# An encoder block on one core: the stages of both latents and of latent attention put in an order worked out from a table of lengths, with products of zeros and ScalarE's loads at the start

## The chip, the core and the metric

The kernel runs on one core of one Trainium2 chip. The metric is the device time of one execution in microseconds (us). Five engines work side by side: TensorE (PE: products and transposes; PEld are its weight loads), VectorE (DVE), ScalarE (ACT), GpSimd (POOL) and SyncE (SP), which only issues transfers here. ScalarE and GpSimd issue transfers too. Each engine works through its own list of instructions in order and waits at each one until its inputs are there.

## What is computed

One layer of a residual block over 512 tokens of width 2048, all in F32. The normalised input is projected once; the columns of the projection feed three branches (a gated short convolution, latent attention, attention to 256 memory tokens) and their gates. What the change touches are the two latents and latent attention:

```python
h = rms_norm(x, norm_g[l]);  proj = h @ w_in[l]          # ... c_q (512), c_kv (512), k_rope_raw (64) ...
q  = (rms_norm(c_q, q_norm_g) @ w_uq).reshape(b, s, 16, 128 + 64)
kv = (rms_norm(c_kv, kv_norm_g) @ w_ukv).reshape(b, s, 16, 128 + 128)
# per head: RMS norm of the 128 and of the 64, rotation of the 64, one shared rotated key,
# scores masked by chunks of 64 tokens, softmax, times values
x = x + merged @ w_o[l]
```

## The kernel before

**Products in three parts.** Every F32 operand is split into a rounded part (`hi`) and the rest (`lo`); `mm3` (lines 124 to 129) makes one product out of three: hi by hi, hi by lo, lo by hi. ScalarE writes the rounded part (line 117), VectorE the rest (line 119, or 121 with a gain). So each chunk of weights costs a transfer (SP), one ScalarE and one VectorE instruction (`forms_of`, lines 220 to 232) before TensorE can use it. Weights come through a ring of 10 tiles (tag `w`) and 6 (`wf`). PSUM has eight banks under two tags, `acc` and `aux`, four each.

**The order of the work.** Stages are lists of steps; `run_range` (lines 263 to 273) makes the next step's forms ahead of this step's products. Line 111 takes SP's queue as written. The order on the other engines comes from a scheduler that keeps its own time line when the program is built; it moves instructions freely past each other where no data forbid it.

**The start.** Lines 146 to 155 load the gains and the identity from ScalarE's queue and run one small activation. Then come the key/value latent's two halves (lines 486 to 533: 8 chunks of 288 columns for half 0, then 8 for half 1; half 0 also loads, splits and squares x, `x_chunk` and `x_squares`, lines 466 to 484), the scale of x (`make_scale`, line 537), and the query latent (line 582: 8 chunks of 512 columns, 24 products each). While these run, x is normalised and cut into the blocks of the next stage (`normalize`, `sums_x`, `build`).

**Latent attention.** The memory heads end with lines 1080 to 1085, then the latents are put into blocks. For each of eight groups of two heads, `keys_values` (line 1113) makes keys and values (48 products of 512 columns) and `queries` (line 1135) the queries (48 products of 384 columns), both out of four banks, with sums of squares, inverse roots on GpSimd (line 136) and scaling. `attend` (line 1182) is one head in four parts: transposes of keys and queries with their splits (`feat`, line 1187), scores and softmax (lines 1206 to 1226), transposes of the probabilities with their splits, the product with the values. Parts are interleaved by strings: `p` is a piece of the projection of the next group, `0` and `1` a part of a head, `L` the last part of the group before:

```python
ORDER_FIRST = "ppppp0p0p0p1p1p0p1"
ORDER = "pp0Lppp01pp01pp01p"
ORDER_LAST = "0p0p1pLp0p1p0p1p1"
```

In the last string `p` is half a step of the next stage, the memory branch's output (lines 1326 to 1328); its inputs are reloaded and split by lines 1410 to 1414. The strings set program order only; the scheduler still moves instructions.

**The end.** `out_group` (line 1385) adds the residual; its last block is stored by one transfer of 512 KB (`put`, line 1393).

Of the kernel before, what the change touches and what calls it, by code (L numbers as in the profile page):

```python
# [43 lines left out]

LINE = 512
SMALL_FILL = 56
# [44 lines left out]

def body(ctx, tc, a, out):
    nc = tc.nc
# [55 lines left out]
    nc.scalar.dma_start(ident, a["ident"])  # L149
# [5 lines left out]
    act.activation(one, one, AF.Copy)  # L155
# [306 lines left out]
    open_work(("q", "b1"))  # L462
    xraw, hx = [None] * 8, [None] * KB
    xacc = []

    def x_chunk(c):
        t = xraw[c] = q("xraw")
        hi, lo = (blk("xhi"), blk("xlo")) if c < 4 else (b1("xhi"), b1("xlo"))
        if c == 0:
            for k in range(KC):  # L470
                nc.sync.dma_start(t[:, k], a["xT"][:, k])
        else:
            nc.sync.dma_start(t, a["xT"][:, KC * c:KC * (c + 1)])
        for k in range(KC):
            split(t[:, k], hi[:, k], lo[:, k], g(G_NORM + KC * c + k))
            hx[KC * c + k] = (hi[:, k], lo[:, k])
# [11 lines left out]

    def kv_forms(n, c):
        if n == 0:  # L490
            x_chunk(c)
        raw = w("raw")
        src = a[f"w_ckv{n}"][c]
        for c0 in range(0, 2 * NK, NK if c == 0 else 2 * NK):
            c1 = c0 + (NK if c == 0 else 2 * NK)
            nc.sync.dma_start(flat(raw)[:, c0:c1], src[:, c0:c1])
        r = forms_of(raw, 2 * NK, c == 0)
        w_done()
        return r

    def kv_products(ws, n, c):
        if c == 0:
            banks_kv[n] = [bank("acc" if n else "aux") for _ in range(NTB)]
        hi, lo = (flat(t)[:, :2 * NK].rearrange("p (k n) -> p k n", k=2) for t in ws)
        for i, k in ([(i, k) for k in range(KC) for i in range(NTB)] if c == 0 else
                     [(i, k) for i in range(NTB) for k in range(KC)]):
# [23 lines left out]
    for n in range(2):  # L530
        for c in range(8):
            steps.append(Step(lambda n=n, c=c: kv_forms(n, c), [lambda ws, n=n, c=c: kv_products(ws, n, c)],
                              [lambda n=n: kv_results(n)] if c == 7 else []))
# [42 lines left out]
    for c in range(8):  # L576
        after(c, lambda c=c: x_squares(c))
    after(7, make_scale)
    for c in range(4):
        after(9 + c, lambda c=c: normalize(c))  # L580
    after(13, lambda: sums_x(0))
# [338 lines left out]
    def rotary_tables():  # L920
        pc, pcr = P2["lat"], P2["latrow"]
        tabs = {}
        pos_i = pcr.tile([P, NTB], I32, name="pos_i")
# [130 lines left out]
    run_all(run_range(0, end_m))  # L1054
# [116 lines left out]
    deep[0] = 0  # L1171
    res0 = {}
# [212 lines left out]
    def out_group(grp):  # L1385
        at = block_of(grp)
        xs = {}

        def early(t, n):
            xs[t, n] = q("x")  # L1390
            nc.gpsimd.dma_start(xs[t, n], at(a["x"], t, n))

        def put(t, n, r):
            nc.scalar.dma_start(at(out, t, n), r)

        def direct(x, r):
            for tt in range(2):
                vec.tensor_tensor(out=r[:, tt], in0=x[tt], in1=xs[0, 0][:, tt], op=ALU.add)
            put(0, 0, r)
        return t_results(put, direct, early, lambda t, n: xs[t, n])  # L1400
# [16 lines left out]
    run(*[{"p": late_steps, "L": late, "0": a0, "1": a1}[c] for c in ORDER_LAST])  # L1417
    close_p()
# [101 lines left out]
```

## Time and profile before

| | us |
|---|---|
| median of 3 runs | 2128.02 (2127.25 to 2128.1) |
| the profiled execution | 2125.74 |
| its span, first to last instruction | 2124.0 |
| TensorE busy | 2089.1 (98%) |
| VectorE busy | 1637.6 (77%) |
| ScalarE busy | 1058.5 (50%) |
| GpSimd busy | 146.0 (7%) |

Busy shares are means over stages with different limits, so they are read by stretches. Ends of products are modelled: a product's record can cover a short wait, so a TensorE that counts as busy can still be slower than in a clean stretch. The granted clock of TensorE has two levels, 1.2 and 2.4 GHz; a share of 0.5 of full speed is the lower one.

### The profile page before, as it was taken

Reading aid. Unit: us, or ns where it says so; the run is one execution under the profiler, and the core shown is the slowest. Engines: PE = TensorE matmul, PEld = TensorE weight load, DVE = VectorE, ACT = ScalarE, POOL = GpSimd, SP = SyncE. Lnnn points to the kernel's source line nnn. Section 1 sums busy time; section 2 is a strip of 40 time slices with the busy share of each in tenths; the row PEclk is TensorE's granted clock in tenths of the full one; section 3 lists DMA queues with packets and bytes.
Section 4 is the critical chain, followed back from the end, with each engine's and each line's share of the span. In section 5 each row is a group of like instructions: output and inputs, shape, how many; then the busy total and the mean of one; then the engine's idle time right before and its main releaser. Section 6 shows DMA issues by size and latency. Waiting matters only on the chain.

```text
span 2124.0 us, 28553 instructions
## 1 busy us (share of the span) xinstructions
PE 2089.1 (98%) x10808; PEld 1797.2 (85%) x10808; DVE 1637.6 (77%) x2162; ACT 1058.5 (50%) x1525; POOL 146.0 (7%) x183
## 2 busy tenths in 40 slices
PE   8999999999999999999999999999999999999999
PEld 8888888887899988898888888888888888888887
DVE  6977788788777777777778788768776688867986
ACT  5454354344444444444356576567665344433543
POOL 0000000000000000000000120312211201111000
PEclk9999999999999999999999999999999999999999
DMA  7456445444443446445556654312232667675672
GB/s 250 132 159 200 136 130 156 132 140 143 164 139 121 149 129 197 145 134 160 165 170 199 230 185 141 112 60 87 85 116 86 261 224 207 210 227 179 200 240 76
DMA packets 106442, 338.64 MB, mean 159 GB/s; under 512 B 11072, under 2 KB 11856, under 8 KB 106304
## 3 DMA queue, kind: packets, MB, share of 16 engines
q1 hardware_dynamic: 71792, 252.21, 37.3%
q0 software_dynamic: 13792, 45.57, 7.2%
q10 hardware_dynamic: 20720, 39.04, 4.9%
q8 instruction: 84, 1.38, 0.3%
q14 instruction: 54, 0.44, 0.1%
HBM read 292.61 MB, written 44.17 MB: 159 GB/s over the span
## 4 chain that ended last, share of the span: by engine, by line
PE 93%; DVE 3%; ACT 2%; issue 1%; DMA 1%; SPq 0%; ACTq 0%; DVEq 0%
PE aux L128 15%; PE aux L127 15%; PE aux L129 15%; PE acc L127 14%; PE acc L128 14%; PE acc L129 14%; PE aux L143 1%; DVE wlo L119 1%; ACT whi L117 1%; PE aux L1232 1%; PE aux L1214 0%; PE aux L1212 0%; PE aux L1213 0%; PE aux L1215 0%; PE aux L1216 0%
## 5 line engine op out<-in xcount | busy, mean ns | idle before, releaser
L117 ACT ACTIVATE whi<-raw 128x1024 fp32r<-128x1024 f32 (+2 forms) x614 | 638.2, 1042 | 848.5 <-PE aux L128 366.0
L119 DVE TENSOR_TENSOR wlo<-raw,whi 128x1024 fp32r<-128x1024 f32 (+2 forms) x614 | 733.2, 1200 | 325.3 <-ACT whi L117 320.2
L366 DVE TENSOR_TENSOR raw<-raw 128x1024 f32<-128x1024 f32 x240 | 293.3, 1223 | 11.5 <-DMA raw<-in_w_mla_out 2.8
L128 PE MATMUL aux<-wlo,f 128*128 128x512 f32 x480 | 187.5, 391 | 1.0 <-DVE wlo L119 0.9
L128 PE MATMUL acc<-wlo,b 128*128 128x512 f32 x480 | 187.3, 390 | 0.0
L129 PE MATMUL aux<-whi,f 128*128 128x512 f32 x480 | 186.9, 389 | 0.0
L128 PE MATMUL aux<-wlo,b 128*128 128x512 f32 x480 | 186.8, 389 | 0.0
L129 PE MATMUL acc<-whi,b 128*128 128x512 f32 x480 | 186.8, 389 | 0.0
L129 PE MATMUL aux<-whi,b 128*128 128x512 f32 x480 | 186.8, 389 | 0.0
L127 PE MATMUL aux<-whi,f 128*128 128x512 f32 x480 | 170.2, 390 | 0.0
L127 PE MATMUL acc<-whi,b 128*128 128x512 f32 x480 | 169.0, 390 | 0.8 <-ACT whi L117 0.7
L127 PE MATMUL aux<-whi,b 128*128 128x512 f32 x480 | 168.1, 390 | 1.4 <-ACT whi L117 1.4
L128 PEld LDWEIGHTS aux<-wlo,f 128*128 128x128 f32 x480 | 90.1, 188 | 21.2 <-DVE wlo L119 2.5
L127 PEld LDWEIGHTS aux<-whi,b 128*128 128x128 f32 x480 | 90.0, 188 | 20.8 <-ACT whi L117 2.3
L127 PEld LDWEIGHTS acc<-whi,b 128*128 128x128 f32 x480 | 89.8, 188 | 20.0 <-ACT whi L117 1.6
L128 PEld LDWEIGHTS aux<-wlo,b 128*128 128x128 f32 x480 | 90.1, 188 | 18.8 <-DVE wlo L119 0.2
L129 PEld LDWEIGHTS aux<-whi,b 128*128 128x128 f32 x480 | 90.1, 188 | 18.7
L128 PEld LDWEIGHTS acc<-wlo,b 128*128 128x128 f32 x480 | 90.1, 188 | 18.7 <-DVE wlo L119 0.2
L129 PEld LDWEIGHTS aux<-whi,f 128*128 128x128 f32 x480 | 90.2, 188 | 18.6
L129 PEld LDWEIGHTS acc<-whi,b 128*128 128x128 f32 x480 | 90.1, 188 | 18.5
L127 PEld LDWEIGHTS aux<-whi,f 128*128 128x128 f32 x480 | 89.9, 188 | 18.8 <-ACT E L1373 0.3
L128 PE MATMUL acc<-wlo,f 128*128 128x512 f32 x240 | 93.4, 389 | 0.0
(393 smaller groups left out, 4502.7 us busy)
## 6 DMA issues: line engine op xcount, KB each, us to landing
raw<-in_w_conv SPq DMA_DIRECT2D x80, 512.0 KB, 4.1
raw<-in_w_gmem SPq DMA_DIRECT2D x44, 512.0 KB, 3.8
raw<-in_w_mla_out SPq DMA_DIRECT2D x44, 512.0 KB, 5.1
raw<-in_w_o SPq DMA_DIRECT2D x44, 512.0 KB, 4.4
raw<-in_w_gconv SPq DMA_DIRECT2D x40, 512.0 KB, 4.2
raw<-in_w_gmla SPq DMA_DIRECT2D x40, 512.0 KB, 3.8
raw<-in_w_mlaz SPq DMA_DIRECT2D x32, 512.0 KB, 4.2
raw<-in_w_mem_kv SPq DMA_DIRECT2D x32, 512.0 KB, 4.5
```

The source lines that it names most:

```text
L117: act.activation(hi, src, AF.Copy, scale=1.0 if g is None else g)
L119: vec.tensor_tensor(out=lo, in0=src, in1=r32(hi), op=ALU.subtract)
L127: nc.tensor.matmul(o, lhsT=s[0], rhs=m[0], start=start, stop=False, skip_group_check=shared)
L128: nc.tensor.matmul(o, lhsT=s[0], rhs=m[1], start=False, stop=False, skip_group_check=shared)
L129: nc.tensor.matmul(o, lhsT=s[1], rhs=m[0], start=False, stop=stop, skip_group_check=shared)
L143: nc.tensor.transpose(out=b[:, i * P:(i + 1) * P], in_=s, identity=ident)
L366: vec.tensor_tensor(out=src_, in0=in0, in1=in1, op=op)
L1232: nc.tensor.transpose(out=b[:, i * P:(i + 1) * P], in_=ps[i][:, j * P:(j + 1) * P], identity=ident)
```

## The change

A class `Player` takes the place of the program object. Outside a recording it passes every call on. In a recording (`start` to `play`) each call is kept with a length out of a small table, with what it reads and writes, and with its tiles. `order` then runs through time: of all instructions whose inputs and tiles are there it takes the one that can start first, among equals the one with the lowest priority number (the place in the program of the earliest product that needs it; for those without one, their own place plus `away`). The result is issued in that order on all five engines, under the fixed-order mode that only SP had before. Two stretches are recorded: from the start to the end of the query latent's products (32 further pieces are recorded to know which tiles are still needed, and then issued as before), and from the first queries of latent attention to the end of `ORDER_LAST`.

At the start five products of a cleared F32 tile (256 columns) stand first. ScalarE's queue loads the first weights' halves; the identity and the small activation come after them. Half 0 and half 1 alternate for their first two chunks. Squares of x come two steps later, the scale two steps later, normalising one step later. At the end the last block is stored in two halves as each is ready. `SMALL_FILL` grows by 8 columns and `pos_i` gets a wider tile in another pool.

```diff
+WARM = 5
+START = 32
-SMALL_FILL = 56
+SMALL_FILL = 64
+class Player:
...
+    def order(self, kept, away=0):
+        ops = self.ops
+        for op in reversed(ops):
+            op.prio = min([op.idx + away] + [s.idx if s.eng == "PE" else s.prio for s in op.succs])
+            if op.eng == "PE":
+                op.prio = op.idx
...
+        while len(out) < len(ops):
+            best = None
+            for e, c in ready.items():
+                for op in c:
+                    at = max(clock[e], op.dep)
+                    need = {}
+                    for t in op.gets:
+                        key = self.first[t][1]
+                        n = need.get(key, 0)
+                        if queue[key][n] != t or len(free[key]) <= n:
+                            at = None
+                            break
+                        at = max(at, sorted(free[key])[n])
+                        need[key] = n + 1
+                    if at is None:
+                        continue
+                    rank = (max(at, clock[e] + SLACK), op.prio)
+                    if best is None or rank < best[0]:
+                        best = rank, op, at
...
+        return sorted(out, key=lambda o: o.at)
+    def play(self, tc, kept, rest=0, away=0):
...
+        with tc.manual_schedule(engines={E.PE, E.DVE, E.Activation, E.Pool, E.SP}):
+            for op in out:
+                op.call()
+        for op in later:
+            op.call()
...
+SEM, SLACK, ROOM, LOAD = 0.05, 0.0, 1.18, 0.0016
+def cost(eng, kind, writes, reads):
+    n = max(int(np.prod(a.shape[1:])) for a in (writes[:1] if kind != "tensor_reduce" else reads))
+    if kind == "dma_start":
+        return {"SP": (max(0.45, n * LOAD), 4.5), "ACT": (0.37, 4.5), "POOL": (0.7, 5.0)}[eng]
+    if eng == "PE":
+        occ = 0.109 if kind == "transpose" else max(n, 136) / 2250
+        return occ, occ + 0.25
+    if eng == "ACT":
+        occ = 0.0009 * n + (0.045 if reads[0].space != bass.MemoryType.PSUM else 0.02)
+        occ += 0.09 * (len(reads) > 1) + 0.1 * (len(writes) > 1)
+    elif eng == "DVE":
+        occ = n / 960 + 0.067 + 0.06 * (kind == "scalar_tensor_tensor")
+    else:
+        occ = 0.33 + 0.165 * n
+    return occ * ROOM, occ * ROOM + 0.2
 def body(ctx, tc, a, out):
-    nc = tc.nc
+    nc = Player(tc.nc)
...
-    nc.scalar.dma_start(ident, a["ident"])
-    act.activation(one, one, AF.Copy)
...
     open_work(("q", "b1"))
+    nc.start()
+    warm, wb = q("warm")[:, 0], bank("acc")
+    vec.memset(warm[:, :HS], 0.0)
+    for _ in range(WARM):
+        nc.tensor.matmul(wb[:, :HS], lhsT=warm[:, :P], rhs=warm[:, :HS], start=True, stop=True)
...
+    def first_forms():
+        raw, src = w("raw"), a["w_ckv0"][0]
+        for c0 in (0, NK):
+            nc.scalar.dma_start(flat(raw)[:, c0:c0 + NK], src[:, c0:c0 + NK])
+        nc.scalar.dma_start(ident, a["ident"])
+        act.activation(one, one, AF.Copy)
+        x_load(0)
+        x_split(0, 0)
+        r = forms_of(raw, NK)
+        x_split(0, 1)
+        split(*(flat(t)[:, NK:2 * NK] for t in (raw, *r)))
+        w_done()
+        return r
...
-    for n in range(2):
-        for c in range(8):
+    for n, c in [(n, c) for c in range(2) for n in range(2)] + [(n, c) for n in range(2) for c in range(2, 8)]:
...
-        after(c, lambda c=c: x_squares(c))
-    after(7, make_scale)
+        after(c + 2, lambda c=c: x_squares(c))
+    after(9, make_scale)
...
-        after(9 + c, lambda c=c: normalize(c))
-    after(13, lambda: sums_x(0))
+        after(10 + c, lambda c=c: normalize(c))
+    after(14, lambda: sums_x(0))
...
-    run_all(run_range(0, end_m))
+    early_steps = run_range(0, end_m)
+    for i in range(first + 16 + START):
+        next(early_steps)
+        if i == first + 15:
+            mark = len(nc.ops)
+    nc.play(tc, (), len(nc.ops) - mark, 100)
+    run_all(early_steps)
...
     deep[0] = 0
+    nc.start()
     res0 = {}
     run_all(queries(0, res0))
...
-            put(0, 0, r)
+                nc.scalar.dma_start(at(out, 0, 0)[:, tt], r[:, tt])
...
     run(*[{"p": late_steps, "L": late, "0": a0, "1": a1}[c] for c in ORDER_LAST])
...
+    nc.play(tc, keep)
```

## Rows read from the trace of the kernel before

**Rows 1.** The page: busy time of the engines over the span, and the chain of waits by engine.
```profile
PE 2089.1 (98%) x10808; PEld 1797.2 (85%) x10808; DVE 1637.6 (77%) x2162; ACT 1058.5 (50%) x1525; POOL 146.0 (7%) x183
...
PE 93%; DVE 3%; ACT 2%; issue 1%; DMA 1%; SPq 0%; ACTq 0%; DVEq 0%
```

**Rows 2.** The table by stretches: from and to in us, length, then busy us and number of instructions of PE, PEld, DVE, ACT and POOL, TensorE's granted clock as a share of full speed, the transfer engines' busy share, GB/s.
```profile
5.00:10.00 5.00, 3.10 (x13) 3.10 (x14) 2.85 (x6) 3.45 (x6) 0.00 (x0) 1.00 0.96 340
10.00:15.00 5.00, 4.76 (x31) 4.53 (x31) 4.86 (x7) 5.00 (x9) 0.00 (x0) 1.00 1.03 414
15.00:20.00 5.00, 5.00 (x40) 5.00 (x40) 5.00 (x8) 5.00 (x9) 0.00 (x0) 1.00 1.03 411
...
100.00:200.00 100.00, 100.00 (x443) 82.80 (x442) 77.97 (x70) 48.52 (x51) 0.00 (x0) 1.00 0.55 174
200.00:1000.00 800.00, 796.58 (x4487) 699.46 (x4486) 618.59 (x578) 368.88 (x387) 0.00 (x0) 1.00 0.46 145
```

**Rows 3.** The time line of the first 7 us: start, length, engine (a q marks an engine's issuing of transfers), line, operation, result and sources; in brackets the idle time before it and what ended that.
```profile
0.74 0.42 ACTq L147 DMA_DIRECT2D gains<-in_gains  x1
...
1.19 0.45 ACTq L149 DMA_DIRECT2D ident<-in_ident  x1
...
1.65 0.90 SPq L496 DMA_DIRECT2D raw<-in_w_ckv  x2
1.67 1.28 ACT L155 ACT_TABLE_LOAD   x1 [1.67 <-PEq L1512]
...
4.23 1.33 ACT L117 ACTIVATE xhi<-xraw,gains 128x512 fp32r<-128x512 f32 x2 [1.06 <-DMA gains<-in_gains]
...
5.47 1.04 ACT L480 ACTIVATE sq<-xraw 128x1024 f32<-128x1024 f32 x1
...
6.42 0.43 ACT L117 ACTIVATE whi<-raw 128x288 fp32r<-128x288 f32 x1
...
6.90 1.33 PE L127 MATMUL aux<-whi,xhi 128*128 128x288 f32 x4 [6.90 <-ACT whi L117]
```

**Rows 4.** Transfers: result and source, issuing queue, count, size, us from issue to landing. The first was issued at 1.65 us and the second at 0.74, the third is the last stores (2080 to 2124 us), the fourth a store of half that size at 1397 to 1399 us.
```profile
raw<-in_w_ckv SPq DMA_DIRECT2D x1, 144.0 KB, 3.7
...
gains<-in_gains ACTq DMA_DIRECT2D x1, 35.0 KB, 3.5
...
out<-r ACTq DMA_DIRECT2D x4, 512.0 KB, 2.7
...
adram<-z ACTq DMA_DIRECT2D x1, 256.0 KB, 2.0
```

**Rows 5.** The table by stretches for latent attention as a whole (from the first key/value product to the last product of the last head) and for two clean pieces of it, one of products of 384 columns and one of 256; then a piece of the chain of waits (start, length, engine, tile, line) with 16 transposes.
```profile
1334.28:1657.50 323.22, 304.50 (x1664) 267.43 (x1665) 232.47 (x677) 207.02 (x505) 67.61 (x81) 0.98 0.27 87
1345.28:1351.20 5.92, 5.92 (x35) 5.92 (x34) 4.96 (x16) 2.37 (x8) 2.93 (x4) 1.00 0.71 232
1403.06:1404.26 1.20, 1.20 (x12) 1.15 (x10) 1.17 (x4) 1.16 (x3) 0.00 (x0) 1.00 0.03 10
...
1972.75 1.75 PE aux L143 x16
```

**Rows 6.** The table by stretches from the first heads of latent attention to its last product.
```profile
1360.00:1370.00 10.00, 7.01 (x39) 5.58 (x37) 7.78 (x20) 8.80 (x22) 2.88 (x3) 0.99 0.25 77
1370.00:1380.00 10.00, 9.94 (x43) 8.70 (x44) 9.81 (x36) 4.36 (x13) 4.00 (x4) 0.84 0.18 54
1380.00:1390.00 10.00, 8.13 (x44) 6.40 (x43) 4.86 (x15) 5.86 (x13) 1.41 (x3) 1.00 0.29 93
1390.00:1400.00 10.00, 8.67 (x44) 7.53 (x45) 5.39 (x18) 5.86 (x16) 1.38 (x2) 0.83 0.19 66
1400.00:1540.00 140.00, 135.62 (x783) 120.90 (x782) 109.28 (x329) 96.78 (x240) 32.07 (x38) 1.00 0.25 77
1540.00:1550.00 10.00, 7.62 (x45) 6.37 (x43) 6.01 (x12) 7.05 (x15) 1.52 (x3) 1.00 0.24 87
1550.00:1560.00 10.00, 9.65 (x50) 9.39 (x51) 7.38 (x24) 6.94 (x21) 2.09 (x3) 0.83 0.36 105
1560.00:1640.00 80.00, 77.08 (x429) 67.35 (x427) 57.65 (x158) 49.60 (x114) 13.09 (x15) 1.00 0.32 106
1640.00:1650.00 10.00, 8.71 (x46) 7.74 (x45) 4.77 (x17) 6.57 (x18) 0.55 (x1) 0.83 0.07 27
1650.00:1657.50 7.50, 6.35 (x34) 5.18 (x33) 1.85 (x5) 1.65 (x5) 0.55 (x1) 1.00 0.09 35
```

**Rows 7.** Pieces of the chain of waits in latent attention: start, length, what the chain was in.
```profile
1358.91 2.93 DMA raw<-in_w_uq
...
1466.99 1.07 ACT whi L117
...
1468.09 1.24 DVE wlo L119
...
1469.35 1.23 DVE wlo L119
...
1540.81 3.76 DMA araw<-adram
```

**Rows 8.** The table by stretches for the products of the first queries alone (the tile cqT), the columns as before without GpSimd.
```profile
1308.50:1329.50 21.00, 9.29 (x48) 8.39 (x48) 0.00 (x0) 0.00 (x0) 1.00 0.40 119
```

**Rows 9.** The time line at the end, VectorE: the last addition.
```profile
2119.53 0.69 DVE L1398 TENSOR_TENSOR r<-acc,x 128x512 f32<-128x512 f32 x1 [0.44 <-PE acc L129]
```

More of the change, by code (lines that the diff above doesn't have):

```diff
@@ new lines, with __init__, __getattr__, call @@
+class Queue:
+    def __init__(self, player, real, eng):
+        self.player, self.real, self.eng = player, real, eng
+    def __getattr__(self, kind):
+        f = getattr(self.real, kind)
+        def call(*args, **kw):
+            if self.player.ops is None:
+                return f(*args, **kw)
+            aps = [(k, v) for k, v in list(enumerate(args)) + list(kw.items()) if hasattr(v, "tensor")]
+            writes = [v for k, v in aps if k in (0, "out", "accum_out")]
+            reads = [v for k, v in aps if k not in (0, "out", "accum_out")]
+            self.player.add(self.eng, lambda: f(*args, **kw), kind, writes, reads)
+        return call
@@ new lines @@
+SEM, SLACK, ROOM, LOAD = 0.05, 0.0, 1.18, 0.0016
[11 more added lines that the diff above has]
+        occ = n / 960 + 0.067 + 0.06 * (kind == "scalar_tensor_tensor")
+    else:
+        occ = 0.33 + 0.165 * n
+    return occ * ROOM, occ * ROOM + 0.2
@@ L462, in body, with x_load, x_split @@
     open_work(("q", "b1"))
+    nc.start()
[3 more added lines that the diff above has]
+        nc.tensor.matmul(wb[:, :HS], lhsT=warm[:, :P], rhs=warm[:, :HS], start=True, stop=True)
     xraw, hx = [None] * 8, [None] * KB
     xacc = []
-    def x_chunk(c):
+    def x_load(c):
         t = xraw[c] = q("xraw")
         hi, lo = (blk("xhi"), blk("xlo")) if c < 4 else (b1("xhi"), b1("xlo"))
-        if c == 0:
-            for k in range(KC):
+        for k in range(KC):
+            hx[KC * c + k] = (hi[:, k], lo[:, k])
+            if c == 0:
                 nc.sync.dma_start(t[:, k], a["xT"][:, k])
-        else:
+        if c:
             nc.sync.dma_start(t, a["xT"][:, KC * c:KC * (c + 1)])
-        for k in range(KC):
-            split(t[:, k], hi[:, k], lo[:, k], g(G_NORM + KC * c + k))
-            hx[KC * c + k] = (hi[:, k], lo[:, k])
+    def x_split(c, k):
+        split(xraw[c][:, k], *hx[KC * c + k], g(G_NORM + KC * c + k))
     def x_squares(c):
@@ L487, in body @@
     banks_kv = {}
+    def first_forms():
[11 more added lines that the diff above has]
+        return r
     def kv_forms(n, c):
+        if n + c == 0:
+            return first_forms()
         if n == 0:
-            x_chunk(c)
+            x_load(c)
+            for k in range(KC):
+                x_split(c, k)
         raw = w("raw")
[L493 to L497, printed above, removed]
+        nc.sync.dma_start(flat(raw)[:, :2 * NK], a[f"w_ckv{n}"][c])
+        r = forms_of(raw, 2 * NK)
         w_done()
@@ L504, in kv_products @@
         hi, lo = (flat(t)[:, :2 * NK].rearrange("p (k n) -> p k n", k=2) for t in ws)
-        for i, k in ([(i, k) for k in range(KC) for i in range(NTB)] if c == 0 else
+        for i, k in ([(i, k) for k in range(KC) for i in range(NTB)] if n + c == 0 else
                      [(i, k) for i in range(NTB) for k in range(KC)]):
@@ L922, in rotary_tables @@
         tabs = {}
-        pos_i = pcr.tile([P, NTB], I32, name="pos_i")
+        pos_i = pcr.tile([P, P], I32, name="pos_i")[:, :NTB]
         nc.gpsimd.dma_start(pos_i, a["pos"])
@@ L1417, in body @@
     run(*[{"p": late_steps, "L": late, "0": a0, "1": a1}[c] for c in ORDER_LAST])
+    ends = {}
+    for t, (op, key, bufs) in nc.first.items():
+        ends.setdefault(t.rsplit("_", 1)[0], []).append(t)
+    keep = {t.tensor.name for t in raws.values()}
+    for n, c in (("whi", 1), ("wlo", 1), ("acc", 4), ("acth", 99), ("actl", 99)):
+        keep.update(ends[n][-c:])
+    nc.play(tc, keep)
     close_p()
```

84 lines of the change are left out of this document (added).

## The prediction

> **What bounds the kernel now.** I read the page's first part and its chain of waits first. TensorE is busy for 2089.1 of 2124.0 us and carries 93% of the chain [rows 1], so nothing off TensorE counts unless it makes TensorE stand, and no change can win more than the time in which TensorE stands or runs slowly. The table by stretches says where that is. Most of the middle is full: from 200 to 1000 us 3.4 of 800 us are idle [rows 2]. Three places are left: the start, latent attention, the end.
>
> *Start.* By 20 us TensorE has run 13 + 31 + 40 = 84 products of 288 columns. At the pace of the last of these stretches (40 in 5.00 us, 0.125 us each) they need 10.5 us, so 9.5 us are lost [rows 2]. Of these, 6.9 us pass before the first product [rows 3]. Most of the rest is the low clock: between 5 and 10 us 13 products take 3.10 us, 0.238 us each, which is 288 columns at 1.2 GHz, although the clock column shows no fall there [rows 2]. The first product waits for the first rounded weights (whi, L117) at 6.42 us. Their transfer was issued at 1.65 us and took 3.7 us, to 5.35 us, but ScalarE was in the square of x (L480, from 5.47 us, 1.04 us) [rows 3, 4].
>
> *Latent attention.* From the first key/value product to the last product of the last head pass 323.2 us [rows 5]. What TensorE needs there is counted from the code and priced by clean stretches of this trace. Products of 512 columns take 0.226 us (443 in 100 us), of 384 columns 0.174 (34 begin in 5.92 us; the row counts one more that overlaps), of 256 columns 0.12 (the row counts 12, ten of which begin in the 1.20 us), transposes 0.109 (16 in 1.75 us) [rows 2, 5]. Keys and values: 384 x 0.226 = 86.8. Queries of seven groups: 336 x 0.174 = 58.5. Scores: 16 heads x 5 x (2 x 0.12 + 0.174 + 0.226) = 51.2. Probabilities times values: 16 x 3 x 0.64 = 30.7. Transposes: 320 x 0.109 = 34.9. Memory output, mixed in: 96 + 17 products, 25.5. Together 287.6, so 35.6 us are lost. The stretches add up to 18.7 us of idle time from 1360 to 1657.5 us (3.0 + 0.1 + 1.9 + 1.3 + 4.4 + 2.4 + 0.3 + 2.9 + 1.3 + 1.2), and four times the granted clock is 0.83 or 0.84 over 10 us, which is half speed for about 1.7 us' worth each, 6.7 us [rows 6]. That is 25.4 us; the other 10.2 us are short waits inside what counts as busy.
>
> *Why it stands there.* In three places the pieces of the chain of waits show an engine held by an instruction that was not urgent [rows 7]: at 1358.9 us a transfer of query weights that ScalarE's order had placed too early, at 1467 us one ScalarE split and two VectorE splits of weights (1.07 + 1.24 + 1.23 us) ahead of the reductions that the next head needed, and at 1540.8 us a reload of memory outputs for 3.8 us. These are faults of order, not of total work: VectorE works 232.5 and ScalarE 207.0 of the 323.2 us [rows 5].
>
> **The change part by part.** The profiled run took 2125.74 us for its span of 2124.0; the median of the runs is 2128.02, 2.3 us above. I make the sum as a difference and take it from the median.
>
> *First loads and square.* The first weights go to ScalarE's queue behind the gains: issued at about 1.19 us, where the identity was issued before, instead of 1.65. With the same 3.7 us they land at 4.89. The rounding of x starts when the gains are there, 0.74 + 3.5 = 4.23 us, as before, and takes 0.67 us for one half; the weights' rounding (0.43) follows without the square, to 5.33, and the first product can start at about 5.5 us [rows 3, 4]. The table load (1.28 us) now follows four issues of about 0.43 us, from about 2.5 to 3.8 us, still before 4.23. If the transfer gains nothing from the other queue it is 5.9 us. Squares two steps later, and key/value halves alternating for two chunks, give VectorE less to do per product early on; it was full from 10 to 20 us [rows 2], so this keeps the pace. SP issues fewer transfers ahead of the next x. I count 0.5 us of small waits.
>
> *Zeros.* One clear of 256 columns on VectorE and five unrounded F32 products on TensorE, at about 1.3 us. No row shows a wide unrounded product. The nearest: a rounded one of 256 columns at half clock, 0.21 us, five in 1.1 us; or F32 transposes, 0.109 us per 128 columns at full clock, 0.44 for 256 at half clock, five in 2.2 us. They would end at 2.4 to 3.5 us and leave TensorE idle before 5.5. If the clock is then still low for 18 products (0.113 us each, 2.0 us), the start gains 9.5 - 5.5 - 0.5 - 2.0 = 1.5 us; if it is up, 3.5. I take 2.5. The ends are 1.1 (late transfer, low clock) and 4.1 us (no small waits). The Trainium skill's page "FP8 and Floating Point Precision", section TensorE Precision Notes, says that true FP32 takes four passes through the array. By that the five take about 4.3 us, up to 5.6, the gap before the first product closes, and the start would gain 3.5 us and the whole 1.0 us more than the sum; no row here shows it.
>
> *Latent attention.* No product, split or transfer is added or removed; every engine's queue, SP's and POOL's included, gets an order found by starting, in a model of lengths, what can start first, and among equals what the earliest product needs. Lengths are 18% above the base values, transfers land after 4.5 or 5 us (the trace: 2.0 to 3.7, rows 4), so a late transfer is placed late. I go by stretches. The opening (1360 to 1400 us: 6.3 idle + 3.4 of clock) has 86.8/8 + 8.3 = 19.2 us of the second group's products that can cover the first heads' chain; I leave 1.5 of 9.7. The middle (1400 to 1640: 10.0 idle + 1.7 clock) can still start a 1.2 us split just ahead of an urgent instruction; I leave 4.0 of 11.7. The last heads (2.4 + 1.7) have only eight half steps of memory output as cover; I leave 2.5 of 4.1. Of the 10.2 us hidden in busy I leave 8.2, since part is the switch between transposes and products. Left 16.2 of 35.6, a gain of 19.4. Bounds: nothing excludes a loss (below); the most is 28.
>
> *Seams.* The block begins at the first queries' products. Before, those 48 (8.3 us) ran from 1309 to 1329 us between the last memory heads [rows 8]. If the block can't be mixed with what stands before it, these heads lose that cover; they keep their own transposes and products of the others, so I count 2.0 us, between 0 and 8.3. At the first block's end VectorE has spare time and I count nothing; the cover is the last chunk's 24 products, 5.4 us, and if it were gone the first gate's two splits (1.07 and 1.23 us) would stand bare. The wider filler tiles cost nothing.
>
> *End.* The last block is stored by halves. The last addition starts at 2119.53 and takes 0.69 us [rows 9]. A 512 KB store lands in 2.7 us, a 256 KB one in 2.0 [rows 4]: 0.7 us, between 0 and 0.7. One more issue (0.4 us) lies under the second addition.
>
> Sum: -2.5 - 19.4 + 2.0 - 0.7 = -20.6, so 2107.4 us by the median, 2105.1 by the profiled run.
>
> **Rivals.** *The chains set the pace, not the order.* Heads wait for four banks that keys, values and queries share, so the same stalls come back in other places and attention gains 4 us: 2128.0 - 2.5 - 4 + 2 - 0.7 = 2122.8. For it: VectorE is at 72% and its chains are long. Against: the named stalls [rows 7] each begin with a split or transfer that could have waited.
>
> *The seam.* All 8.3 us of the query products leave their cover, and the clock falls once (1.7): 10.0 instead of 2.0, 2115.4 us. For it: the block is closed in the code. Against: much of the cover is the memory heads' own.
>
> *Slower: a split ahead of each group's first head.* The rule starts whatever can start and holds nothing back for an urgent instruction. If every group's key chain meets one ScalarE and two VectorE splits of weights, as at 1467 us (3.5 us) [rows 7], with nothing on TensorE to cover them, then 16.2 + 8 x 3.5 = 44.2 are lost against 35.6: 8.6 more, with the other terms (-1.2) 2135.4 us. It decides from (35.6 - 16.2 + 1.2 + 4.3)/8 = 3.1 us per group. For it: VectorE works on splits half of the time. Against: the order prefers the earliest product's needs among those ready.
>
> **How the numbers follow.** The forecast has 0.70, the chains 0.12, the seam 0.09, the slower case 0.09. I predict 2107.4 us. The forecast's own range is 2098 to 2117; reaching to the seam and nearly to the chains, the range is 2097 to 2121 us. 0.2%, 4.3 us, is about what a measurement here can tell from no change. Faster: the forecast, the seam and half of the chains, 0.85. Same: the other half and a small part of the slower case, 0.07. Slower 0.08.
>
> **What would show it.** Right: products at 0.13 us from the first one, which comes near 5.5 us; idle time from the opening to 1640 us below a third of now, with no fall of the granted clock; no weight split or transfer on the chain just before a key or query transpose; the last store landing 0.7 us sooner. Wrong: a first product after 6.5 us; idle TensorE between the last memory heads and the first queries (the seam); waits for weight splits in each group (the slower case); the same idle sum with other names (the chains).

## The result and the profile after

| | before | after |
|---|---|---|
| median of 4 runs, us | 2127.64 (2125.81 to 2128.1) | 2102.07 (2100.8 to 2102.35) |
| profiled execution / its span, us | 2125.74 / 2124.0 | 2101.8 / 2100.0 |

The ratio is 0.988, with a 95% interval of 0.9863 to 0.9897: 25.6 us less by the medians, 24.0 by the profiled executions, against 20.6 forecast. In the page after the change (busy time, then the chain of waits by engine) TensorE is at 99% and on 95% of the chain, against 98% and 93% in [rows 1]:

```profile
PE 2083.3 (99%) x10818; PEld 1795.1 (85%) x10818; DVE 1642.5 (78%) x2162; ACT 1057.7 (50%) x1524; POOL 150.5 (7%) x183
...
PE 95%; DVE 2%; ACT 1%; issue 1%; DMA 1%; POOL 0%; ACTq 0%; DVEq 0%; POOLq 0%
```

Every call now passes through the recorder, so all lines read L233 (passed on) or L237 (recorded); the rows are read by their tiles.

**By stretches.** The table of the kernel after (columns as in rows 2), answering to [rows 2, 6]:

```profile
5.00:10.00 5.00, 4.67 (x27) 3.72 (x25) 3.72 (x6) 3.99 (x7) 0.00 (x0) 1.00 1.04 379
10.00:15.00 5.00, 4.12 (x29) 3.89 (x30) 2.98 (x5) 3.63 (x6) 0.00 (x0) 1.00 0.97 361
15.00:20.00 5.00, 5.00 (x40) 5.00 (x39) 2.96 (x5) 2.82 (x6) 0.00 (x0) 1.00 1.00 362
1320.00:1330.00 10.00, 8.18 (x46) 6.17 (x44) 6.40 (x10) 4.39 (x10) 2.39 (x4) 1.00 0.70 183
1330.00:1340.00 10.00, 8.97 (x38) 8.35 (x39) 8.32 (x24) 7.55 (x12) 3.05 (x3) 0.83 0.52 189
1340.00:1370.00 30.00, 30.00 (x153) 26.00 (x152) 24.03 (x56) 18.66 (x49) 8.00 (x9) 1.00 0.27 93
1370.00:1380.00 10.00, 8.04 (x40) 6.70 (x39) 8.57 (x27) 8.59 (x19) 2.06 (x3) 0.83 0.13 40
1380.00:1400.00 20.00, 20.00 (x117) 17.56 (x117) 16.20 (x45) 11.37 (x30) 3.96 (x5) 1.00 0.33 112
1400.00:1640.00 240.00, 239.32 (x1376) 214.90 (x1376) 186.75 (x539) 166.16 (x402) 59.99 (x71) 1.00 0.30 97
1640.00:1655.00 15.00, 15.00 (x68) 12.42 (x67) 10.57 (x15) 6.59 (x8) 0.72 (x1) 1.00 1.03 414
```

From 1400 to 1640 us 0.7 us are idle, where [rows 6] had 10.0. Most of what is left of the loss stands in two places, each with one fall of the granted clock behind it: 1328 to 1335 us, the seam, and 1373 to 1379, the opening.

Idle time alone misses what a product's record covers. So I also took, product by product, the distance from one start to the next, less the clean pace of its width (0.2275 us for 512 columns, 0.1733 for 384, 0.1195 for 256, 0.109 for a transpose). That sum is the loss of a stretch, the low clock included:

| loss in us | before | after | forecast left |
|---|---|---|---|
| seam (1320 to 1360) | 0.9 | 5.8 | +2.0 |
| opening (1360 to 1400) | 11.6 | 4.6 | 1.5 of 9.7 visible |
| middle (1400 to 1640; after: to 1612) | 18.8 | 3.5 | 4.0 of 11.7 visible |
| last heads (1640 to 1670; after: 1612 to 1640) | 5.0 | 0.3 | 2.5 of 4.1 visible |
| hidden | in the rows above | in the rows above | 8.2 of 10.2 |
| sum from 1280 | 36.5 | 14.3 | 18.2 |

The rows go by the work and not by the hour: after the change the last head's scores begin at 1613.3 us and its last product at 1631.3, so what stands at 1640 us in the table of stretches is the stage behind it. The sums hold the 0.2 us from 1280 to 1320, too. The forecast's count by hand, 35.6 us lost, agrees with the 36.5 of this measure.

**The start.** The time line of the kernel after, answering to [rows 3]:

```profile
1.19 0.45 ACTq L237 DMA_DIRECT2D raw<-in_w_ckv  x1
...
1.25 4.63 PE L237 MATMUL acc<-warm 128*128 128x256 f32 x10 [1.25 <-DVE invd L233]
...
5.03 0.44 ACT L237 ACTIVATE whi<-raw 128x288 fp32r<-128x288 f32 x1 [1.39 <-DMA raw<-in_w_ckv]
5.12 0.34 ACTq L237 DMA_DIRECT2D raw<-in_w_ckv  x1
...
5.38 0.71 ACT L237 ACTIVATE xhi<-xraw,gains 128x512 fp32r<-128x512 f32 x1
...
6.14 0.61 PE L237 MATMUL aux<-whi,xhi 128*128 128x288 f32 x1 [0.25 <-ACT xhi L237]
```

The five zero products fill TensorE from 1.25 to 5.88 us (each counts as two records). The first product starts at 6.14 instead of 6.90, and it waits for xhi, not for whi: the list put the weights first, and ScalarE stood 1.39 us until they landed. The second half of the same weights is issued only at 5.12 us, just after the first half has landed. The 80th product (the zeros not counted) begins at 18.57 us instead of 19.98, and a stall in the middle that stood at 509.5 us now stands at 507.4, so the start gave 2.1 us in these profiles, 1.4 of them by the 80th product. This is sure to about 1 us only: in the profiled executions of other kernels below that begin with the same recorded start, the 80th product begins between 17.71 (start_only) and 18.73 us (the listed kernel run again).

**The seam and the opening.** Time line of the kernel after, TensorE and ScalarE at the seam, then TensorE and VectorE at the opening:

```profile
1326.84 1.59 PE L233 MATMUL aux<-ident,ckv 128*128 128x128 f32 x12
...
1328.34 0.37 ACTq L233 DMA_DIRECT2D adram<-z  x1
1328.76 0.69 ACT L233 ACTIVATE ckT<-aux,gains 128x512 fp32r<-128x512 f32 x1
1329.35 0.30 ACT L237 ACTIVATE pt30h<-zero 128x128 fp32r<-128x128 f32 x1
...
1330.15 2.72 ACT L237 ACTIVATE whi<-raw 128x768 fp32r<-128x768 f32 x3
1331.03 1.43 PE L237 MATMUL acc<-whi,cqT 128*128 128x384 f32 x4 [2.60 <-ACT whi L237]
...
1372.55 1.27 PE L237 MATMUL aux<-ident,s 128*128 128x128 f32 x7
1374.58 0.42 DVE L237 TENSOR_TENSOR qn<-acc,rs_r 128x256 f32<-128x256 f32 x1
1374.91 1.48 DVE L237 TENSOR_TENSOR ptl<-aux,pth 128x512 fp32r<-128x512 f32 x3
1375.65 1.11 PE L237 MATMUL aux<-ident,kn 128*128 128x128 f32 x4 [1.83 <-DVE ptl L237]
```

At the seam TensorE stands 2.60 us for the first split of the block, behind the last key block, a store and four copies of zeros in ScalarE's queue. At the opening the next key's transposes wait 1.83 us for a bank that VectorE's ptl empties. Both gaps are followed by some 3.4 us of products at half pace.

**The end.** From the last addition to the end of the span pass 3.98 us (2096.02 to 2100.0) instead of 4.47 [rows 9]; a half store now lands in 2.3 us, in the view of transfers:

```profile
2096.02 0.69 DVE L233 TENSOR_TENSOR r<-acc,x 128x512 f32<-128x512 f32 x1 [0.44 <-PE acc L233]
```

```profile
out<-r ACTq DMA_DIRECT2D x2, 512.0 KB, 2.7
out<-r ACTq DMA_DIRECT2D x2, 256.0 KB, 2.3
```

### The profile page after: what moved, and what is told of

Read it like the earlier page. It is cut to its first block, busy times and chain, and to the rows that moved or that the text cites. A ratio compares the mean times of both kernels' runs of the same rounds, so it can differ in the third digit from the quotient of the medians.

```text
span 2100.0 us, 28564 instructions
## 1 busy us (share of the span) xinstructions
PE 2083.3 (99%) x10818; PEld 1795.1 (85%) x10818; DVE 1642.5 (78%) x2162; ACT 1057.7 (50%) x1524; POOL 150.5 (7%) x183
## 3 DMA queue, kind: packets, MB, share of 16 engines
q8 instruction: 85, 1.39, 0.3%
## 4 chain that ended last, share of the span: by engine, by line
PE 95%; DVE 2%; ACT 1%; issue 1%; DMA 1%; POOL 0%; ACTq 0%; DVEq 0%; POOLq 0%
PE aux L233 40%; PE acc L233 33%; PE aux L237 12%; PE acc L237 10%; DVE wlo L233 0%; DMA raw<-in_w_ckv 0%; DVE cv L233 0%; DVE raw L233 0%; ACT whi L233 0%; DMA raw<-in_w_mla_out 0%; DMA raw<-in_w_memz 0%; ACT s L237 0%; DVE ss L237 0%; DVE r L233 0%; DVE s L233 0%
## 5 line engine op out<-in xcount | busy, mean ns | idle before, releaser
L233 ACT ACTIVATE whi<-raw 128x1024 fp32r<-128x1024 f32 x521 | 550.5, 1060 | 765.2 <-PE aux L233 347.6
L233 DVE TENSOR_TENSOR wlo<-raw,whi 128x1024 fp32r<-128x1024 f32 x521 | 633.6, 1222 | 285.9 <-ACT whi L233 281.7
L233 DVE TENSOR_TENSOR raw<-raw 128x1024 f32<-128x1024 f32 x258 | 315.2, 1223 | 10.3 <-DMA raw<-in_w_mla_out 3.4
L233 PE MATMUL aux<-whi,b 128*128 128x512 f32 x896 | 293.3, 389 | 1.4 <-ACT whi L233 1.4
L233 PE MATMUL aux<-whi,f 128*128 128x512 f32 x880 | 289.7, 390 | 0.0
L233 PE MATMUL acc<-whi,b 128*128 128x512 f32 x880 | 287.1, 390 | 0.8 <-ACT whi L233 0.7
L233 PEld LDWEIGHTS aux<-whi,b 128*128 128x128 f32 x896 | 168.0, 188 | 37.0 <-ACT whi L233 2.3
L233 PEld LDWEIGHTS acc<-whi,b 128*128 128x128 f32 x880 | 164.9, 188 | 35.5 <-ACT whi L233 1.6
L233 PEld LDWEIGHTS aux<-whi,f 128*128 128x128 f32 x880 | 165.0, 188 | 34.3 <-ACT E L233 0.3
L233 PE MATMUL aux<-wlo,b 128*128 128x512 f32 x448 | 174.3, 389 | 0.0
L233 PE MATMUL aux<-wlo,f 128*128 128x512 f32 x440 | 171.9, 391 | 1.0 <-DVE wlo L233 0.9
L233 PE MATMUL acc<-wlo,b 128*128 128x512 f32 x440 | 171.8, 390 | 0.7 <-DVE wlo L233 0.7
L233 PE MATMUL acc<-whi,f 128*128 128x512 f32 x448 | 140.5, 389 | 0.0
L237 DVE TENSOR_TENSOR wlo<-raw,whi 128x1024 fp32r<-128x1024 f32 (+3 forms) x92 | 99.1, 1084 | 29.2 <-ACT whi L237 24.9
L237 ACT ACTIVATE whi<-raw 128x1024 fp32r<-128x1024 f32 (+3 forms) x92 | 86.6, 951 | 63.3 <-PE acc L237 23.0
L233 PEld LDWEIGHTS aux<-wlo,f 128*128 128x128 f32 x440 | 82.6, 188 | 19.4 <-DVE wlo L233 2.2
L233 PEld LDWEIGHTS aux<-wlo,b 128*128 128x128 f32 x448 | 84.1, 188 | 17.6 <-DVE wlo L233 0.2
L233 PEld LDWEIGHTS acc<-whi,f 128*128 128x128 f32 x448 | 84.1, 188 | 17.5
L233 PEld LDWEIGHTS acc<-wlo,b 128*128 128x128 f32 x440 | 82.6, 188 | 18.1 <-DVE wlo L233 1.2
L233 PE MATMUL acc<-wlo,f 128*128 128x512 f32 x224 | 87.1, 389 | 0.0
L233 PE MATMUL acc<-whi,mT 128*128 128x512 f32 x256 | 80.8, 392 | 0.0
L233 POOL DMA_DIRECT2D mraw<-in_memT x4 | 2.2, 552 | 1082.5 <-DMA gdram<-r 1061.2
```

Source lines behind the costliest of these rows:

```text
L233: return f(*args, **kw)
L237: self.player.add(self.eng, lambda: f(*args, **kw), kind, writes, reads)
```

## The experiments

Three groups of four kernels; the kernel before was run beside each group (medians 2126.56, 2125.77 and 2126.8 us), and every ratio is to it.

**1. The start alone.** The second block's recording and the stores by halves are undone.

```diff
-    nc.start()
     res0 = {}
...
-                nc.scalar.dma_start(at(out, 0, 0)[:, tt], r[:, tt])
+            put(0, 0, r)
...
-    nc.play(tc, keep)
```

> The first recorded block, the zeros and ScalarE's loads as in the change; latent attention and the last store as before. The middle of the changed kernel runs 2.1 us earlier than before (the stall at 509.5 us stands at 507.4), so if the parts add up: 2127.6 - 2.1 = 2125.5 us (2124.5 to 2126.5). Rival, that the start is worth more and latent attention less (the two disturb each other): below 2123.

Measured: 2123.82 us, ratio 0.9987 (0.9978 to 0.9996), 2.7 us less than before. The time itself lies 0.7 us under the range that I had given, since the kernel before ran 1.1 us lower beside it, too; the difference is the size of the start's term (2.1 to 2.7).

**2. Latent attention alone.** All edits of the start and the stores by halves are undone.

```diff
-WARM = 5
-START = 32
...
-    early_steps = run_range(0, end_m)
...
-    nc.play(tc, (), len(nc.ops) - mark, 100)
+    run_all(run_range(0, end_m))
```

> Only the second recorded block (latent attention to the end of the last string); start and last store as before. If the list order of this block is the source: 2127.6 - 22 to 23 = 2105 us (2103.5 to 2106.5), with idle time of TensorE only at the seam (about 2.6 us) and in the opening (about 2 us). Rival, that the gain needs the changed start or its shift: above 2112.

Measured: 2104.22 us, ratio 0.9897 (0.9883 to 0.991): 22.3 us less. With the 2.7 of the start the parts give 25.0 of the whole's 25.6; the stores by halves are in neither, and the rest is within the runs' spread. The chains rival (4 us from attention) falls.

**3. The block closed, but in the order written.**

```diff
-        out = self.order(lambda t: t in used or t in kept, away)
+        out = self.order(lambda t: t in used or t in kept, away) if listed else list(self.ops)
...
-    nc.play(tc, keep)
+    nc.play(tc, keep, listed=False)
```

> The changed kernel, but the second block is issued in the order in which the program makes it, fixed on all engines, without the list. If the list makes the gain: each head's softmax and each group's roots then stand ahead of the next products on every engine, some 16 heads x 3 us and more lost, 2150 us or above. Rival, that it is enough to take this stage out of the scheduler's hands: 2101 to 2106.

Measured: 2475.93 us, ratio 1.1645 (1.163 to 1.1661). The stretch of the block by the table, and the waits from 1500 to 1900 us:

```profile
1400.00:1900.00 500.00, 279.96 (x1217) 233.95 (x1215) 184.78 (x518) 162.99 (x386) 47.51 (x60) 0.74 0.11 35
```

```profile
PE acc L237 <- ACT whi L237: 99.3, 19, 7.3
ACT kTh L237 <- PE aux L237: 90.8, 5, 18.3
ACT pth L237 <- PE aux L237: 82.3, 9, 10.6
...
PE acc L237 <- DVE wlo L237: 50.5, 18, 8.9
```

(A row has the sum in us, how many, the longest.) Splits of weights now end TensorE's waits, up to 8.9 us at a time, and the granted clock is 0.74 on the mean. The splits come late because ScalarE, taking its list as written, first waits for the heads' transposes (kTh, pth), up to 18.3 us. So fixing an order gains nothing by itself: the gain is what `order` puts into the list. This is the reverse of the forecast's slower rival, which had a split ahead of urgent work; here the split is the urgent work and stands behind a head's.

**4. No zeros** (`-WARM = 5`, `+WARM = 0`).

> The changed kernel without the five products of zeros. If they are there for the clock: the first 18 products run at 1.2 GHz, 18 x 0.113 = 2.0 us more, 2104.1 us (2103.3 to 2104.6), products 0.24 us apart until about 10.5 us. Rival, that TensorE waits for data in these microseconds anyway: 2102.1 to 2102.6.

Measured: 2103.99 us, ratio 0.9894 (0.988 to 0.9907), 1.9 us above the listed kernel. Its first 15 us:

```profile
5.00:10.00 5.00, 3.39 (x14) 3.39 (x15) 3.08 (x5) 3.46 (x6) 0.00 (x0) 1.00 1.00 362
10.00:15.00 5.00, 5.00 (x34) 4.81 (x33) 3.17 (x5) 4.16 (x6) 0.00 (x0) 1.00 1.04 364
```

14 products run in the 5 us where the listed kernel begins 24 (its other records there are zeros), and they start 0.24 us apart until 11.1 us. With the zeros they start 0.13 us apart from about 7 us on. So the zeros do bring the higher clock forward. What that is worth is less sure than the 1.9 us: the 80th product begins at 19.49 us, 0.9 later than in the listed kernel, and the stall near 509 us is 0.9 later, too; the rest of what this profiled execution lost (2.6 us in all) lies behind 1670 us, far from the start. The two ratios' intervals overlap.

**5. The second load not held for the first.** The list lets every later instruction on a tile wait for the tile's first one, here the landing of the first half's load. In this kernel a later load that has no other reason to wait follows the first one's issue. A second edit goes with it: loads on ScalarE's queue land after 4.9 us in the table instead of 4.5.

```diff
-                elif self.first[t.name][0] is not op:
+                elif self.first[t.name][0] is not op and self.first[t.name][0] not in op.preds:
                     op.preds.add(self.first[t.name][0])
+                    op.soft.add(self.first[t.name][0])
...
-s.dep = max(s.dep, at + (op.lat + SEM if far or s.eng != op.eng else op.occ))
+s.dep = max(s.dep, at + (op.occ if op in s.soft else op.lat + SEM if far or s.eng != op.eng else op.occ))
...
-        return {"SP": (max(0.45, n * LOAD), 4.5), "ACT": (0.37, 4.5), "POOL": (0.7, 5.0)}[eng]
+        return {"SP": (max(0.45, n * LOAD), 4.5), "ACT": (0.37, 4.9), "POOL": (0.7, 5.0)}[eng]
```

> The changed kernel, but in the list a second load into a tile no longer waits for the first to land, and ScalarE's transfers are taken as 4.9 us. In the changed kernel the second halves of x and of the first weights were issued at 4.28 and 5.12 us. If that is why the start gained less than possible: first product at 5.9 us when the zeros end, no stalls between 10 and 12 us, 1.5 us less than the changed kernel, 2100.6 us (2099.8 to 2101.2). Rival, that the transfers' rate in the first 10 us sets this: no more than 0.4 us less.

Measured: 2100.31 us, ratio 0.9875 (0.986 to 0.989), 1.5 us under the listed kernel run beside it (2101.77 us, ratio 0.9884, 0.987 to 0.9897). The table shows where:

```profile
5.00:10.00 5.00, 5.00 (x30) 4.33 (x29) 3.91 (x7) 3.65 (x7) 0.00 (x0) 1.00 1.02 381
10.00:15.00 5.00, 5.00 (x39) 5.00 (x39) 4.14 (x6) 4.77 (x8) 0.00 (x0) 1.00 1.03 407
```

From 10 to 15 us TensorE is full (39 products, 29 in the listed kernel), the first product starts at 5.72 us, since xhi now stands ahead of whi, and the 80th at 17.03. Which of the two edits does it, this run alone can't say. Run 11 below has the edit on tiles with the 4.5 left as it was:

```profile
5.00:10.00 5.00, 2.85 (x19) 2.31 (x17) 2.38 (x5) 2.86 (x6) 0.00 (x0) 1.00 0.97 340
10.00:15.00 5.00, 5.00 (x39) 4.91 (x38) 4.22 (x7) 5.00 (x8) 0.00 (x0) 1.00 1.03 395
```

There ScalarE stands for the weights again, the first product starts at 6.28 us, TensorE then waits 1.17 us before 9.30, and the 80th product begins at 18.46 us, within the range of the listed kernel's starts. So the rule on tiles explains the listed kernel's 0.88 us of idle time between 10 and 15 us, but without it the wait only moves ahead of 10 us; the gain goes with the order of x and weights that the 4.9 gives, or with how fast the first loads land. These runs don't part the two.

**6. The table trusts the loads.** Landings in the second block's table are 0.5 us, and 1.0 for GpSimd's, instead of 4.5 and 5.0.

```diff
+LAND = [4.5]
...
-        return {"SP": (max(0.45, n * LOAD), 4.5), "ACT": (0.37, 4.5), "POOL": (0.7, 5.0)}[eng]
+        return {"SP": (max(0.45, n * LOAD), LAND[0]), "ACT": (0.37, LAND[0]), "POOL": (0.7, LAND[0] + 0.5)}[eng]
...
+    LAND[0] = 0.5
     nc.start()
```

> The changed kernel, but for the second block the list takes transfers as landed after 0.5 us (1.0 from GpSimd) instead of 4.5 and 5.0. If the long landing times in the table are what keeps a late transfer from blocking a queue: stalls behind weights and reloads come back, 4 to 12 us more, 2106 to 2114 us. Rival, that any list of this kind serves (transfers are issued far ahead in both): 2101 to 2103.5.

Measured: 2113.91 us, ratio 0.994 (0.9928 to 0.9953), 12 us slower than the listed kernel. Its largest stall, which with the low clock behind it holds 6.4 us of the loss (1440 to 1455 us; 0.2 in the listed kernel), on the time line:

```profile
1443.38 0.59 POOL L237 DMA_DIRECT2D z<-zdram  x1 [7.90 <-DMA adram<-z]
1444.00 0.72 POOL L237 TENSOR_TENSOR rs_r<-rs_t,mhalf 128x2 f32<-128x2 f32 x1
1444.75 0.63 ACT L237 ACTIVATE kn<-acc,rs_r 128x128 f32<-128x128 f32 x2 [4.77 <-POOL rs_r L237]
...
1445.43 0.69 PE L237 MATMUL acc<-whi,cqT 128*128 128x384 f32 x1 [3.45 <-ACT kn L237]
```

Read it upwards from TensorE: the product waits for a bank that ScalarE's kn empties, kn waits for GpSimd's power, and the power stands in GpSimd's queue behind an issue of a load, which waits 7.90 us until a store has landed and freed its tile. With landings at 0.5 us in the table that issue looked free; with 4.5 us for the store the list mostly puts such issues where the wait is over: of the twelve loads of z that GpSimd issues from 1400 to 1610 us, one waits in the listed kernel (3.54 us) and eleven here (0.67 to 10.96 us). The long landings, by which the forecast only had late loads placed late, are what keeps the engines' queues clear.

**7. Two chunks of the first queries' weights split ahead of the block**, to take the split at the seam away.

```diff
-    ready_forms = [chunk_forms(a["w_uq"][0][0], 384)]
+    ready_forms = [chunk_forms(a["w_uq"][0][c], 384) for c in range(2)][::-1]
```

> The changed kernel, with the second chunk of the first queries' weights split before the second block. If the seam is ScalarE doing the last key blocks, four copies of zeros and then this split (2.6 us idle at 1328 us) and the low clock that follows (1.7 us): 4 us less, 2098 us (2097 to 2099.3), and no fall of the granted clock near 1331 us. Rival, that TensorE waits there for key blocks or banks: the gap moves to the next products, 2101.5 to 2102.5.

Measured: 2103.78 us, ratio 0.9895 (0.9881 to 0.9908): 2.0 us slower by the medians, where 3.8 less was expected (1.7 us of it would be a longer fall of the clock in the profiled execution, 6.8 us instead of 3.4; the intervals overlap). The miss is mine: I had taken the named split for the cause. Its time line:

```profile
1329.26 1.91 PE L233 MATMUL aux<-ident,ckv 128*128 128x128 f32 x16
...
1332.99 1.06 ACT L237 ACTIVATE whi<-raw 128x1024 fp32r<-128x1024 f32 x1
...
1334.10 0.50 PE L237 MATMUL aux<-whi,ckT 128*128 128x512 f32 x1 [2.94 <-ACT whi L237]
1335.37 0.80 PE L237 MATMUL aux<-wlo,ckT 128*128 128x512 f32 x1 [0.76 <-DVE wlo L237]
```

All query products are done between the memory heads, and TensorE now stands 2.94 us for the next split, that of the keys' weights, a longer one. Whichever product comes next, it waits for ScalarE's queue: key blocks, zero copies, then the first split recorded in the block.

**8 to 11. The seam taken apart.** The key blocks recorded ahead of the last two memory heads (keys_early), those heads' stores on GpSimd's queue instead of ScalarE's (store_pool), both (keys_store), and both with the edit of 5 on tiles, but ScalarE's landings left at 4.5 us (keys_store_soft).

```diff
     query_blocks()
+    key_blocks()
     for h in range(2, 4):
         run_all(heads_m[h])
-    key_blocks()
```

```diff
-        nc.scalar.dma_start(two(adram, 2 * head), z)
+        (nc.gpsimd if head >= 2 else nc.scalar).dma_start(two(adram, 2 * head), z)
```

> The listed kernel, with the four key blocks recorded ahead of the last two memory heads rather than after them. In the listed kernel TensorE is idle for 2.60 us at 1328.4 and then runs 3.4 us at the low clock (4.3 us in all). Theory A, ScalarE's queue as a whole holds the seam: the key blocks leave its end, but the last memory head's store still stands in that queue and waits for VectorE's product of TensorE's last bank (0.69 us), and behind it come 0.37 us of store, 0.8 us of zero copies and 0.9 us of the first split, 2.8 us after the last product; so the gap stays 2 to 3 us and the time 2101 to 2102.5. Rival B, the key blocks alone hold it: the gap goes, and the time falls by some 4 us to 2097.5 to 2098.5.

> The listed kernel, with the stores of the last two memory heads issued on GpSimd's queue instead of ScalarE's. Theory A, ScalarE's queue as a whole: the last key split still ends at about 1329, and the zero copies and the first split follow, so only the store's own 0.4 us goes: gap 2.1 to 2.4 us, time 2101 to 2102. Rival C, the store alone holds the seam: the gap goes, 2097.5 to 2098.5.

> Both edits together: key blocks early, last two stores on GpSimd's queue. Theory A: nothing that waits for TensorE's last memory product is left ahead of the first split, which runs some 3 us earlier, so the idle 2.6 us and the low clock behind it (1.7 us) go: 2097.3 to 2098.5, and the first excess in the block is at the opening. Rival D, another engine ends the wait next (VectorE's key remainders, or the remainder wlo of the split): at most 1.5 us of gain, 2100.3 or more.

> Both edits of the seam, and the start's second loads not held for the first ones in the list (which by itself gave 1.5 us). The two lie 1300 us apart, so the gains add by theory A: 2095.8 to 2097. Rival D: the start's 1.5 us and at most 1.5 us more, 2098.8 or more.

| | median us | ratio (95%) | idle at the seam, us |
|---|---|---|---|
| keys_early | 2102.3 | 0.9882 (0.9867 to 0.9896) | 3.01 |
| store_pool | 2101.92 | 0.9884 (0.9868 to 0.9901) | 2.30 |
| keys_store | 2099.61 | 0.9872 (0.9857 to 0.9887) | 1.36 |
| keys_store_soft | 2098.61 | 0.9867 (0.9852 to 0.9881) | 1.36 |

Neither edit alone changes the listed kernel's median (2102.07, and 2101.77 run again) by more than 0.5 us, as theory A had it. (Their profiled executions are the shortest of their runs, and in them the granted clock does not fall at the seam. In keys_early its mean is 1.000 there and 0.998 in the other three executions, which are 1.9 to 2.9 us longer.) With the key blocks gone, the last store holds ScalarE, since it waits for VectorE's product of TensorE's last bank. The time line of keys_early:

```profile
1328.23 0.39 PE L233 MATMUL aux<-ph,mvl 128*128 128x512 f32 x1
...
1329.53 0.37 ACTq L233 DMA_DIRECT2D adram<-z  x1
1329.94 0.31 ACT L237 ACTIVATE pt30h<-zero 128x128 fp32r<-128x128 f32 x1 [3.96 <-DVE z L233]
...
1331.63 0.97 PE L237 MATMUL acc<-whi,cqT 128*128 128x384 f32 x4 [3.01 <-ACT whi L237]
```

Both together gain about half of the 4.3 us that I expected: 1.7 to 2.6 us by the ratios (0.9872 against 0.988 and 0.9884), with intervals that overlap, so that even this gain is not clear of the spread. 2099.61 us lies between theory A (at most 2098.5) and rival D (2100.3 or more), whose reason, another wait behind the first, is what the trace has. The gap is 1.36 us, and the time line of keys_store says what is late next:

```profile
1327.77 0.31 ACT L237 ACTIVATE pt30h<-zero 128x128 fp32r<-128x128 f32 x1 [1.76 <-PE aux L233]
1328.48 0.39 PE L233 MATMUL aux<-ph,mvl 128*128 128x512 f32 x1
1328.74 0.31 ACT L237 ACTIVATE pt30l<-zero 128x128 fp32r<-128x128 f32 x1 [0.66 <-PE aux L233]
...
1329.36 2.73 ACT L237 ACTIVATE whi<-raw 128x768 fp32r<-128x768 f32 x3
1330.24 0.98 PE L237 MATMUL acc<-whi,cqT 128*128 128x384 f32 x4 [1.36 <-ACT whi L237]
```

The copies of zeros, which have no input to wait for, wait for TensorE's last memory products, 1.76 and 0.66 us. From the code the likely reason is memory: the pool of latent attention's tiles is opened where memory attention's pools were closed, so the first tiles written there wait for the last readers of what lay there. Behind the second wait 0.6 us of copies and the split follow, 1.5 us in all. That it is the place in memory was not tried by moving it. keys_store_soft, the shortest of all, is 2.8 to 3.6 us under the listed kernel by the ratios (0.9867 against 0.988 and 0.9884), but over the 2097 that theory A allowed. Its 1.0 us under keys_store is within the spread, and its profiled execution does not show it at the start: the 80th product begins at 18.46 us against 18.62.

## Why the prediction was right

*Mechanism and sign: right.* The middle's stalls were faults of order, and a list that models time takes them away (2, 3, 6). 2102.07 us lies 5.3 us under the forecast and inside its own range of 2098 to 2117. That it lies so near owes something to luck: latent attention's gain was forecast 7.6 us too small and the seam's cost 2.9 us too small, and the two errors work against each other. Which engine's order gave how much, SP's among them, no run here shows.

*The signs.* Idle time from the opening to 1640 us fell below a third, as forecast (2.6 of 16.3 us). But the clock still fell once there, the first products ran 0.25 us apart until 7.0 us and came at 6.14, and one sign of being wrong did show: TensorE idle between the last memory heads and the first queries, 2.60 us, the seam.

*Latent attention, 19.4 us: mis-sized, 27.0.* From the opening to the last heads the loss fell from 35.4 to 8.4 us by the rows of the table; with the seam it fell by 36.5 - 14.3 = 22.2 us, where the forecast had 19.4 - 2.0 = 17.4 (experiment 2 measured 22.3). Within that the terms were off both ways. The middle is left with 3.5 us in all, hidden waits included, where 4.0 visible and most of 8.2 hidden were left; the last heads with 0.3 instead of 2.5. The argument "part of the hidden 10.2 us is the switch between transposes and products, so it stays" failed: the clean stretches after the change lose 0.1 to 0.2 us in 10 with the same switches in them, so most of it had been short waits. The opening was the other way, 4.6 us left instead of 1.5 visible: next keys' transposes wait for a bank that the heads' probabilities fill and VectorE empties. A shared bank behind a chain is what the chains rival had, and it is true in this one place; the bank is of tag `aux` there, and the queries before and the keys behind write `acc`.

*Seam, +2.0: mis-sized, 4.9.* Its ends (0 to 8.3) held it, its mechanism was only half seen. I counted query products that lose their cover, but the list's first ones still ran between the memory heads. What the closed block costs is that the list begins as if all queues were empty, so it does not know of the key block and the store that ScalarE still has to do (8 to 10), nor, as is likely but not shown, of the memory that its copies wait for. The clock fell once behind it, as the seam rival priced it.

*Slower: a split ahead of each group's first head.* It did not come. A poor list does cost time in this block, but by other waits: splits behind a head's work (3), issues that wait (6). Its landings of 4.5 to 5 us keep waiting issues off the queues.

*Start, 2.5: right in size (2.1 in the profiles, 2.7 by experiment 1), with one step wrong.* (Its upper end should be 4.0 and not 4.1: 9.5 - 5.5.) The first product came at 6.14 us, not near 5.5: the order whi, xhi was assumed the other way round, and ScalarE stood 1.39 us for the transfer. The zeros took 4.63 us, above the 1.1 to 2.2 us that the rows bounded and near the 4.3 us worked out from the Trainium skill's page "FP8 and Floating Point Precision", section TensorE Precision Notes, by four passes; the trace agrees with the page, and the transposes were a bad neighbour row to choose. The 3.5 us that went with it did not come: products waited again behind them, 0.88 us between 10 and 15 us alone. The zeros bring the clock up earlier (4); their worth is 0.9 us in the traces and 1.9 by the medians, against the 2.0 that the forecast put between a low and a high clock.

*End, 0.7: 0.49 measured,* since a half store lands in 2.3 us here and not in 2.0.

## What to carry to other kernels

A stall whose releaser is a split or a load that could have waited is worth an order worked out from lengths; whether it pays lies in the lengths for transfers: here lengths above the landings of the block (4.5 and 5.0 us against medians of 2.0 to 4.1) served, and 0.5 and 1.0 cost 12 us, since an issue that waits holds every instruction behind it on its engine. A block with a fixed order has edges: look for what the queues still hold when it begins, and let the list start from there. When a gap's releaser is moved and the gap only changes its name, as with two chunks ready, read the releaser's whole queue back to the last instruction that had to wait.

## What the runs showed of the hardware

- An F32 product of 256 columns that is not rounded took 0.93 us at the start (4.63 us for five, while products were still at half pace: the next ones begin 0.25 us apart until 7.0 us), against 0.12 for a rounded one at the full clock [rows 5]: a wide F32 product is no cheap filler where the gap is short.
- Whether the clock fell behind a gap did not follow the gap's length. The granted clock was at half for 3.4 us behind the listed kernel's 2.60 and 1.83 us, for 6.8 us behind two_ready's 2.94, and not at all at the seam in the profiled executions of keys_early (3.01), store_pool (2.30) and keys_store (1.36). Nor was it the same in each execution of one kernel (keys_early, above). So the 1.7 us that I used per gap throughout is the price of one such fall; whether there is none, one or two has to be seen in the trace.
- One recorded start, run in several kernels, had its 80th product at 17.71 to 18.73 us: in these microseconds, where the transfer engines' busy share is 0.96 to 1.04 (5 to 20 us), a difference under 1 us between two single profiles shows little.
